# Low-part score products over 128 rows in place of 64, in a hybrid attention encoder on one Trainium2 core

## The chip, the cores and the metric

The kernel runs on one core of one Trainium2 chip. The metric is device time of one execution in microseconds (us). Engines are called as in the profile: PE is TensorE (PEld its weight loads), DVE is VectorE, ACT is ScalarE, POOL is GpSimd, SP is SyncE, which issues the DMAs here.

## What is computed

Two layers, each with three attention branches side by side over 512 tokens of width 1024. Two of the branches matter here, the banded one (8 heads on 2 key/value heads, 64 wide, each query block of 128 sees its own and its neighbour blocks) and the differential one (4 heads, two components of 64 each):

```python
def swa_branch(q, k, v, sink, bias_band):
    ...
    s = jnp.einsum('bnqgrd,bnkgd->bngrqk', q, kb).astype(jnp.float32) * SWA_HEAD_DIM ** -0.5
    s = s + bias_band.reshape(SWA_KV_HEADS, SWA_GROUP, BLOCK, 3 * BLOCK)[None, None]
    ...
    m = jnp.maximum(jnp.max(s, axis=-1, keepdims=True), sink_l)
    p = jnp.exp(s - m)
    p = p / (jnp.sum(p, axis=-1, keepdims=True) + jnp.exp(sink_l - m))
    ...

def diff_branch(q, k, v, lam_q1, lam_k1, lam_q2, lam_k2, g_sub, rel_bias, lam_init):
    ...
        s = jnp.einsum('bqhcd,bkhcd->bchqk', qb, k).astype(f32) * d ** -0.5 + bias[None, None]
        p = jax.nn.softmax(s, axis=-1)
        a = p[:, 0] - lam * p[:, 1]
        return jnp.einsum('bhqk,bkhe->bqhe', a.astype(v.dtype), v)
    ...

for l in range(DEPTH):
    ...
    o_a = (mla_branch(...) * jax.nn.silu(za)) @ w_o_mla[l]
    o_b = (swa_branch(qb_, kb_, vb_, sink[l], swa_bias) * jax.nn.silu(zb)) @ w_o_swa[l]
    o_c = (diff_branch(...) * jax.nn.silu(zc)) @ w_o_diff[l]
    y = (g[:, :, 0] * o_a + g[:, :, 1] * o_b + g[:, :, 2] * o_c) @ w_out[l]
    x = x + gate * rms_norm(y, g_post[l])
```

## The kernel before

Every float32 operand of a product is split in two parts that PE takes as float32r: a high part, the rounded copy made by ACT (`act_copy`, L81), and a low part, the rest, made by DVE (`sub`, L84). A product is then three matmuls into one PSUM tile (`mm3`, L86 to L89): high by high, high by low, low by high. A weight unit (`wunit`, L100) is a DMA of 512 KB into a `wr` tile (2 buffers), ACT's split into `wh` and DVE's into `wl` (3 buffers each). A projection (`proj_T`, L451) takes one unit and 24 matmuls of 512 columns.

The scores of the two branches have heads of only 64 rows, half of PE's height, and use it so: `stack_q` (L786) puts the high query of a head in one half of the 128 partitions and its low part in the other half; `stack_k` (L798) puts the high key in both halves, the second by a DVE copy (L802). One matmul over 128 rows is then high key by high query plus high key by low query. The third term, low key by high query, is a second matmul into the same score tile over the 64 rows of the high query alone.

- Banded branch (`swa_attention`, L839): for 2 key heads, 4 query blocks and 4 query heads, L866 is the first product and L867 the second, 256 columns wide for the outer blocks and 384 for the inner ones: 32 pairs per layer. The low key is made in `swa_kv` (L822), which also copies it into the other half (L823), since a key head serves query heads of both halves.
- Differential branch (`diff_attention`, L923): for 4 heads, 4 query tiles and 2 components, L939 is the first product and L940 the second, 512 columns: 32 pairs per layer. The low keys of both components share one tile `kl`, a half each, made in `diff_qkv` (L905, L916).

Score tiles rotate through 2 PSUM buffers (`sc`). DVE adds the bias and takes the maximum (L868, L941), ACT the exponential (L874, L946), POOL scales (L882, L950). Then `second` transposes the probabilities (L691) and multiplies them by the values (L700 to L704, `mm3`). Queries and keys lie in tiles of the tag `op`, a ring of 12 buffers; a differential head took 5 of them (2 queries, 2 high keys, 1 for the low keys).

The order of the instructions on each engine is fixed when the program is built, by a scheduler that works with estimated times and with the priorities set in the code (`tc.high_priority`); between the score products stand projections, merges (`merge_steps`) and, in layer 0, pieces of the next layer's modulation (`mod_late`, `mod_rows`), whose weights go through the same `wr` ring.

Of the kernel before, what the change touches and what calls it, by code (L numbers as in the profile page):

```python
# [12 lines left out]
F32R = mybir.dt.float32r  # L13
# [4 lines left out]
P = 128  # L18
S = 512
# [31 lines left out]
def hybrid_kernel(ctx, tc, x, c, w_ada, b_ada, g_pre, g_post, w_in, g_q, w_uq, g_kv, w_ukv,  # L51
# [6 lines left out]
    pe, act, dve, pool, sp = nc.tensor, nc.scalar, nc.vector, nc.gpsimd, nc.sync  # L58
# [4 lines left out]
    def T(tag, shape, dt=F32, bufs=None):  # L63
        count[0] += 1
        return sb.tile(shape, dt, tag=tag, name=f"{tag}_{count[0]}",
                       bufs=bufs or BUFS.get(tag, 1))

    def stat(n):
        return T("st", [P, n], F32, 24)
# [3 lines left out]
    def Q(tag):  # L73
        count[0] += 1
        return ps.tile([P, S], F32, tag=tag, name=f"ps_{tag}_{count[0]}", bufs=PB[tag])

    def f(ap):
        return ap.bitcast(F32)

    def act_copy(out_, in_, scale=1.0):  # L80
        return act.activation(out=out_, in_=in_, func=AF.Copy, scale=scale)  # L81

    def sub(out_, a, b, eng=None):
        return (eng or dve).tensor_tensor(out=out_, in0=a, in1=b, op=ALU.subtract)  # L84
# [69 lines left out]
    for k, src, n in ((PR_GQ, g_q, 2), (PR_GKV, g_kv, 1), (PR_GSUB, g_sub, 1)):  # L154
        pool.dma_start(out=prm[1][k - 32:k - 32 + n * DEPTH, :],
                       in_=src.rearrange("l (a b) -> (l a) b", b=P))
# [118 lines left out]
    def bg_step(n=1):  # L275
        for _ in range(n):
            if bg and next(bg[0], bg) is bg:
                bg.clear()
# [163 lines left out]
    def skewed(d2, pitch, n):  # L442
        a = d2[0:1, :]
        return bass.AP(tensor=a.tensor, offset=a.offset + 127, ap=[[pitch, P], [1, n]])
# [243 lines left out]
    def transposed_block(blocks):  # L688
        tr = Q("tr")
        for i, b in enumerate(blocks):  # L690
            pe.transpose(tr[:, i * P:(i + 1) * P], b, ident)  # L691
        ph = T("pt", [P, S], F32R)
        pl = T("pt", [P, S], F32R)
        act_copy(ph, tr)
        sub(pl, tr, f(ph))
        return ph, pl
# [142 lines left out]
    def swa_attention(l, qs, kk, vt):  # L839
        o_all = []  # L840
        bt = []

        def first(idx):
            g, n = idx // NT, idx % NT
            kh, kl = kk[g]
            if n == 0:
                bt.clear()
                for i in range(2):
                    b = T("x5", [P, 896])
                    for h in range(2):  # L850
                        sp.dma_start(out=b[:, h * 384:(h + 1) * 384],
                                     in_=skewed(bias_s[4 * g + 2 * i + h], 511, 384))
                    bt.extend([b[:, 0:384], b[:, 384:768]])
                o_all.extend(T("o", [P, S]) for _ in range(2))
            k0, k1 = max(n - 1, 0), min(n + 2, NT)
            j0 = (k0 - n + 1) * P
            w = (k1 - k0) * P
            mx, sm, nm, sk, rr = (stat(4) for _ in range(5))
            pr = T("p", [P, NT, S])
            for i in range(4):  # L860
                q = qs[4 * g + i]
                hi = slice((i % 2) * 64, (i % 2) * 64 + 64)
                s = Q("sc")
                ts_ = slice(n * P, (n + 1) * P)
                ks_ = slice(k0 * P, k1 * P)
                pe.matmul(s[:, :w], q[:, ts_], kh[:, ks_], start=True, stop=False)  # L866
                pe.matmul(s[:, :w], q[hi, ts_], kl[hi, ks_], start=False, stop=True)  # L867
                dve.tensor_tensor_reduce(  # L868
                    out=pr[:, i, :w], in0=s[:, :w], in1=bt[i][:, j0:j0 + w], scale=1.0,
                    scalar=sinkt[:, l * 8 + 4 * g + i:l * 8 + 4 * g + i + 1],  # L870
                    op0=ALU.add, op1=ALU.max, accum_out=mx[:, i:i + 1])
                dve.tensor_scalar(out=nm[:, i:i + 1], in0=mx[:, i:i + 1], scalar1=-1.0,
                                  scalar2=None, op0=ALU.mult)
                act.activation(out=pr[:, i, :w], in_=pr[:, i, :w], func=AF.Exp,  # L874
                               bias=nm[:, i:i + 1], accum_out=sm[:, i:i + 1])
            dve.tensor_tensor(out=sk, in0=sinkt[:, l * 8 + 4 * g:l * 8 + 4 * g + 4], in1=nm,
                              op=ALU.add)
            act.activation(out=sk, in_=sk, func=AF.Exp)
            dve.tensor_tensor(out=sk, in0=sk, in1=sm, op=ALU.add)
            dve.reciprocal(out=rr, in_=sk)  # L880
            for i in range(4):
                pool.tensor_scalar(out=pr[:, i, :w], in0=pr[:, i, :w], scalar1=rr[:, i:i + 1],  # L882
                                   scalar2=1.0, op0=ALU.mult, op1=ALU.mult)
            return pr

        def second(idx, pr):
            g, n = idx // NT, idx % NT
            ob = o_all[2 * g:2 * g + 2]
            k0, k1 = max(n - 1, 0), min(n + 2, NT)
            av = Q("av")  # L890
            for kb in range(k0, k1):
                ph, pl = transposed_block([pr[:, i, (kb - k0) * P:(kb - k0 + 1) * P]
                                           for i in range(4)])
                av_step(av, vt[:, kb * 2 + g], ph, pl, kb == k0, kb == k1 - 1)
            ol = T("ta", [P, S])
            act_copy(ol[0:64], av[64:128])
            for i in range(4):
                dve.tensor_tensor(out=ob[i // 2][(i % 2) * 64:(i % 2) * 64 + 64, n * P:(n + 1) * P],
                                  in0=av[0:64, i * P:(i + 1) * P],
                                  in1=ol[0:64, i * P:(i + 1) * P], op=ALU.add)  # L900

        pipelined(first, second, 2 * NT)
        return o_all

    def diff_qkv(l, hd, hh, hl):  # L905
        bg_step()
        qq = stack_q(l, C_QC + hd * P, hh, hl)
        bg_step()
        kh = [T("op", [P, S], F32R) for _ in range(2)]
        kl = T("op", [P, S], F32R)  # L910
        ka = proj_T(l, C_KC + hd * P, hh, hl)
        for i in range(2):
            stack_k(ka, i, kh[i])
        for i in range(2):
            hi = slice(i * 64, i * 64 + 64)
            sub(kl[hi], ka[hi], f(kh[i][hi]))  # L916
        vt = T("big", [P, 2, S], F32R)
        tr = v_transposed(proj_T(l, C_VC + hd * P, hh, hl))
        act_copy(vt[:, 0], tr)
        sub(vt[:, 1], tr, f(vt[:, 0]))  # L920
        return qq, kh, kl, vt

    def diff_attention(l, hh, hl, fill):  # L923
# [3 lines left out]
        def first(hd):  # L927
            qq, kh, kl, vt = ops[hd]
            b = T("x5", [P, 896])
            sp.dma_start(out=b, in_=skewed(bias_d[hd], 1023, 896))  # L930
            pr = T("p", [P, NT, S])
            for t in range(NT):
                ts_ = slice(t * P, (t + 1) * P)
                mx, nm, sm, rr = (stat(2) for _ in range(4))
                pc = [pr[:, t], T("ta", [P, S])]
                for i in range(2):
                    hi = slice(i * 64, i * 64 + 64)
                    s = Q("sc")
                    pe.matmul(s, qq[i][:, ts_], kh[i], start=True, stop=False)  # L939
                    pe.matmul(s, qq[i][hi, ts_], kl[hi], start=False, stop=True)  # L940
                    dve.tensor_tensor_reduce(out=pc[i], in0=s, in1=b[:, 384 - t * P:896 - t * P],  # L941
                                             scale=1.0, scalar=-3.0e38, op0=ALU.add, op1=ALU.max,
                                             accum_out=mx[:, i:i + 1])
                    dve.tensor_scalar(out=nm[:, i:i + 1], in0=mx[:, i:i + 1], scalar1=-1.0,  # L944
                                      scalar2=None, op0=ALU.mult)
                    act.activation(out=pc[i], in_=pc[i], func=AF.Exp, bias=nm[:, i:i + 1],  # L946
                                   accum_out=sm[:, i:i + 1])
                dve.reciprocal(out=rr, in_=sm)
                dve.tensor_tensor(out=rr[:, 1:2], in0=rr[:, 1:2], in1=lam_neg[l], op=ALU.mult)
                pool.tensor_scalar(out=pc[1], in0=pc[1], scalar1=rr[:, 1:2], scalar2=1.0,  # L950
                                   op0=ALU.mult, op1=ALU.mult)
                dve.scalar_tensor_tensor(out=pc[0], in0=pc[0], scalar=rr[:, 0:1], in1=pc[1],
                                         op0=ALU.mult, op1=ALU.add)
            return pr
# [244 lines left out]
```

## Time and profile before

| what | us |
|---|---|
| median of 3 timed runs | 1256.59 (1256.41 to 1256.79) |
| span of the profiled execution | 1256.0; its time with what lies around the span isn't listed apart |
| PE matmul L87, L88, L89 into `ps_dn` from `hT` (840 each) | 339.8, 336.3, 335.7 |
| PE transposes L691 (544) | 94.1 |
| DVE weight splits L84 `wl` (141) | 179.5 |
| ACT weight splits L81 `wh` (141) | 149.1 |

The page divides the span in 40 slices; these rows give the busy share of each engine in tenths, and the clock that PE was granted in tenths of full speed:

```profile
PE   5898999999999999999999999999999999999997
DVE  7864676986765577665567558778765557766553
PEclk8899999999999999999999999999999999999999
```

The banded branch of layer 0 lies in slices 8 to 12, the differential one in 14 to 18; layer 1 follows from slice 21 on. A row of a timeline gives start, duration, engine, line, operation, output <- inputs, rows*columns of the stationary operand, the moving operand's shape. Matmuls are pipelined, so the duration of one overlaps its neighbours, and the distance of two starts is the time that a matmul takes in the stream. "Idle before" is the time the engine stood still ahead of an instruction, with what ended it; "issue" there is idle time that ended with nothing the profile shows.

### The profile page before, as it was taken

The numbers are of one execution on the slowest core, as the hardware profiler recorded it, in microseconds if no ns is written. First come the engines' busy times: TensorE is split into PE (matmuls) and PEld (weight loads), VectorE is DVE, ScalarE is ACT, GpSimd is POOL, SyncE is SP. The second block draws the span as 40 slices with busy tenths as digits, with TensorE's granted clock in tenths as the row PEclk, the third lists the DMA queues.
The fourth block names the chain that finished last, engine by engine and source line by source line (L and its number), as shares of the span: only waits on it lengthen the run. The fifth ranks groups of instructions, "written<-read, shape, count | busy, mean of one in ns | idle before, by whom it ended". The sixth has DMA issues, their size and how long they took to land.

```text
span 1256.0 us, 15558 instructions
## 1 busy us (share of the span) xinstructions
PE 1216.1 (97%) x5428; PEld 944.4 (75%) x5428; DVE 837.2 (67%) x1732; ACT 632.2 (50%) x1250; POOL 188.3 (15%) x238
## 2 busy tenths in 40 slices
PE   5898999999999999999999999999999999999997
PEld 4776787767777767787878888887777876777786
DVE  7864676986765577665567558778765557766553
ACT  5454565545543446554357446564544345565431
POOL 4400211211110010001131001221121001000123
PEclk8899999999999999999999999999999999999999
DMA  9648431354355232334454433224422332223442
GB/s 317 186 123 233 118 99 55 102 149 143 94 144 160 77 85 70 96 96 137 133 173 132 110 92 87 63 80 134 126 68 81 100 93 74 82 84 86 142 156 95
DMA packets 169523, 146.86 MB, mean 117 GB/s; under 512 B 7679, under 2 KB 146999, under 8 KB 169444
## 3 DMA queue, kind: packets, MB, share of 16 engines
q1 hardware_dynamic: 169316, 145.85, 40.1%
q8 instruction: 43, 0.70, 0.2%
q14 instruction: 36, 0.29, 0.1%
q0 software_dynamic: 128, 0.01, 0.0%
HBM read 135.83 MB, written 14.20 MB: 119 GB/s over the span
## 4 chain that ended last, share of the span: by engine, by line
PE 81%; DVE 7%; DMA 6%; ACT 2%; POOL 2%; issue 1%; SPq 1%; DVEq 0%; POOLq 0%; ACTq 0%
PE ps_dn L87 18%; PE ps_dn L88 18%; PE ps_dn L89 18%; PE ps_tr L691 5%; DMA wr<-in_w_in 4%; PE ps_sc L940 2%; DVE o L202 2%; PE ps_sc L87 2%; PE ps_sc L89 2%; PE ps_sc L88 2%; PE ps_sc L867 2%; PE ps_av L701 1%; PE ps_av L700 1%; PE ps_sc L939 1%; DVE wl L84 1%
## 5 line engine op out<-in xcount | busy, mean ns | idle before, releaser
L87 PE MATMUL ps_dn<-hTh,wh 128*128 128x512 f32 x840 | 339.8, 404 | 2.6 <-ACT tf L479 1.8
L88 PE MATMUL ps_dn<-hTl,wh 128*128 128x512 f32 x840 | 336.3, 400 | 0.0
L89 PE MATMUL ps_dn<-hTh,wl 128*128 128x512 f32 x840 | 335.7, 400 | 0.4 <-DVE wl L84 0.4
L84 DVE TENSOR_TENSOR wl<-wr,wh 128x1024 fp32r<-128x1024 f32 x141 | 179.5, 1273 | 137.9 <-ACT wh L81 135.0
L81 ACT ACTIVATE wh<-wr 128x1024 fp32r<-128x1024 f32 x141 | 149.1, 1058 | 187.7 <-PE ps_dn L88 117.9
L87 PEld LDWEIGHTS ps_dn<-hTh,wh 128*128 128x128 f32 x840 | 158.3, 188 | 43.9 <-issue 6.4
L89 PEld LDWEIGHTS ps_dn<-hTh,wl 128*128 128x128 f32 x840 | 158.2, 188 | 38.3 <-issue 1.5
L88 PEld LDWEIGHTS ps_dn<-hTl,wh 128*128 128x128 f32 x840 | 158.3, 189 | 37.3 <-issue 2.8
L81 ACT ACTIVATE pt<-ps_tr 128x512 fp32r<-128x512 f32 x136 | 79.0, 596 | 91.9 <-PE ps_tr L691 91.2
L84 DVE TENSOR_TENSOR pt<-ps_tr,pt 128x512 fp32r<-128x512 f32 x136 | 92.1, 685 | 38.9 <-ACT pt L81 37.8
L691 PE MATMUL ps_tr<-ident,p 128*128 128x128 f32 x544 | 94.1, 275 | 1.0 <-POOL p L762 1.0
L762 POOL TENSOR_SCALAR p<-p,st 128x512 f32<-128x512 f32 x64 | 49.0, 783 | 291.2 <-DVE st L760 254.0
L691 PEld LDWEIGHTS ps_tr<-ident,p 128*128 128x128 f32 x544 | 68.9, 141 | 23.9 <-issue 3.3
L87 PE MATMUL ps_dn<-u,wh 128*128 128x512 f32 x192 | 77.4, 403 | 1.8 <-DVE x L298 1.8
L89 PE MATMUL ps_dn<-u,wl 128*128 128x512 f32 x192 | 77.3, 402 | 0.0
L88 PE MATMUL ps_dn<-u,wh 128*128 128x512 f32 x192 | 77.2, 402 | 0.0
L950 POOL TENSOR_SCALAR ta<-ta,st 128x512 f32<-128x512 f32 x32 | 22.9, 716 | 338.0 <-DVE st L944 207.4
L882 POOL TENSOR_SCALAR p<-p,st 128x256 f32<-128x256 f32 (+1 forms) x64 | 38.2, 616 | 185.9 <-DVE st L880 161.2
L758 ACT ACTIVATE p<-ps_sc,st 128x512 f32<-128x512 f32 x64 | 43.8, 686 | 36.3 <-DVE st L757 36.0
L757 DVE TENSOR_REDUCE st<-ps_sc 128x1 f32<-128x512 f32 x64 | 43.4, 686 | 15.8 <-PE ps_sc L89 15.4
L87 PEld LDWEIGHTS ps_dn<-u,wh 128*128 128x128 f32 x192 | 36.1, 188 | 11.7 <-DVE x L298 2.6
L868 DVE CUSTOM_DVE_ANT_0 p<-ps_sc,x,sinkt 128x256 f32<-128x256 f32 (+1 forms) x64 | 34.0, 545 | 16.2 <-PE ps_sc L867 12.0
(345 smaller groups left out, 2119.8 us busy)
## 6 DMA issues: line engine op xcount, KB each, us to landing
wr<-in_w_in SPq DMA_DIRECT2D x105, 512.0 KB, 3.9
wr<-in_w_ada SPq DMA_DIRECT2D x32, 512.0 KB, 3.7
wr<-in_w_out SPq DMA_DIRECT2D x16, 512.0 KB, 3.7
big<-in_w_ada SPq DMA_DIRECT2D x10, 512.0 KB, 9.3
big<-in_x SPq DMA_DIRECT2D x8, 512.0 KB, 4.9
wr<-in_w_o_mla SPq DMA_DIRECT2D x8, 512.0 KB, 3.6
wr<-in_w_o_swa SPq DMA_DIRECT2D x8, 512.0 KB, 3.5
wr<-in_w_o_diff SPq DMA_DIRECT2D x8, 512.0 KB, 3.4
```

Source lines behind the costliest of these rows:

```text
L81: return act.activation(out=out_, in_=in_, func=AF.Copy, scale=scale)
L84: return (eng or dve).tensor_tensor(out=out_, in0=a, in1=b, op=ALU.subtract)
L87: pe.matmul(o, ah, bh, start=start, stop=False)
L88: pe.matmul(o, ah, bl, start=False, stop=False)
L89: pe.matmul(o, al, bh, start=False, stop=stop)
L202: end = dve.scalar_tensor_tensor(out=acc, in0=src[k], scalar=cact[:, k:k + 1], in1=acc, op0=ALU.mult, op1=ALU.add)
L691: pe.transpose(tr[:, i * P:(i + 1) * P], b, ident)
L757: dve.tensor_reduce(out=nm[:, t:t + 1], in_=s, axis=AX.X, op=ALU.max, negate=True)
L758: act.activation(out=pr[:, t], in_=s, func=AF.Exp, bias=nm[:, t:t + 1], accum_out=sm[:, t:t + 1])
L762: pool.tensor_scalar(out=pr[:, t], in0=pr[:, t], scalar1=rr[:, t:t + 1], scalar2=1.0, op0=ALU.mult, op1=ALU.mult)
L868: dve.tensor_tensor_reduce(out=pr[:, i, :w], in0=s[:, :w], in1=bt[i][:, j0:j0 + w], scale=1.0, scalar=sinkt[:, l * 8 + 4 * g + i:l * 8 + 4 ...
L882: pool.tensor_scalar(out=pr[:, i, :w], in0=pr[:, i, :w], scalar1=rr[:, i:i + 1], scalar2=1.0, op0=ALU.mult, op1=ALU.mult)
```

## The change

The second product of both branches runs over all 128 rows. In the banded branch that only drops the selection of rows, since the low key lay in both halves already. In the differential branch `kl` becomes two tiles, one per component, and a DVE copy puts each low key into the other half too: 2 more copies of 64x512 and 1 more `op` tile per head (6 in place of 5). With the low key in both halves, the second product also adds low key by low query, which the kernel before left out.

```diff
@@ swa_attention, first
             for i in range(4):
                 q = qs[4 * g + i]
-                hi = slice((i % 2) * 64, (i % 2) * 64 + 64)
                 s = Q("sc")
...
                 pe.matmul(s[:, :w], q[:, ts_], kh[:, ks_], start=True, stop=False)
-                pe.matmul(s[:, :w], q[hi, ts_], kl[hi, ks_], start=False, stop=True)
+                pe.matmul(s[:, :w], q[:, ts_], kl[:, ks_], start=False, stop=True)
@@ diff_qkv
         kh = [T("op", [P, S], F32R) for _ in range(2)]
-        kl = T("op", [P, S], F32R)
+        kl = [T("op", [P, S], F32R) for _ in range(2)]
...
         for i in range(2):
             hi = slice(i * 64, i * 64 + 64)
-            sub(kl[hi], ka[hi], f(kh[i][hi]))
+            lo = slice(64 - i * 64, 128 - i * 64)
+            sub(kl[i][hi], ka[hi], f(kh[i][hi]))
+            dve.tensor_copy(out=kl[i][lo], in_=f(kl[i][hi]))
@@ diff_attention, first
                 for i in range(2):
-                    hi = slice(i * 64, i * 64 + 64)
                     s = Q("sc")
                     pe.matmul(s, qq[i][:, ts_], kh[i], start=True, stop=False)
-                    pe.matmul(s, qq[i][hi, ts_], kl[hi], start=False, stop=True)
+                    pe.matmul(s, qq[i][:, ts_], kl[i], start=False, stop=True)
```

The change also moves instructions, from the start of the differential branch on; ahead of it no engine's order changes. Three places follow; lines of the banded branch are one lower in the code after, those of `diff_attention` are the same, and the new copy is L917.

First, PE at the first scores of head 0 in layer 0 (out <- moving, stationary; op_3712 and op_3713 are the queries, op_3752 and op_3753 the high keys, op_3754 and, after, op_3755 the low keys). Before:

```order
L89 MATMUL ps_dn_3799<-hTh_119,wl_3795 128x512
L939 MATMUL ps_sc_3965<-op_3752,op_3712 128x512
L939 MATMUL ps_sc_3971<-op_3753,op_3713 128x512
L940 MATMUL ps_sc_3965<-op_3754,op_3712 128x512
L87 MATMUL ps_dn_3844<-hTh_119,wh_3839 128x512
```

After, the same place:

```order
L89 MATMUL ps_dn_3802<-hTh_119,wl_3798 128x512
L939 MATMUL ps_sc_3971<-op_3752,op_3712 128x512
L939 MATMUL ps_sc_3977<-op_3753,op_3713 128x512
L87 MATMUL ps_dn_3847<-hTh_119,wh_3842 128x512
L88 MATMUL ps_dn_3847<-hTl_120,wh_3842 128x512
```

And after, 48 matmuls of two projections later:

```order
L89 MATMUL ps_dn_3889<-hTh_119,wl_3885 128x512
L940 MATMUL ps_sc_3971<-op_3754,op_3712 128x512
L940 MATMUL ps_sc_3977<-op_3755,op_3713 128x512
L87 MATMUL ps_dn_3929<-hTh_119,wh_3924 128x512
L88 MATMUL ps_dn_3929<-hTl_120,wh_3924 128x512
```

The first second product moved behind these two projections, to where the second one of the same tile pair stood before.

Second, DVE at the keys of head 0 in layer 0, from the copies of the high key on. Before:

```order
L802 CAST op_3752<-op_3752 64x512
L802 CAST op_3753<-op_3753 64x512
L84 TENSOR_TENSOR op_3754<-ps_dn_3761,op_3752 64x512
L84 TENSOR_TENSOR op_3754<-ps_dn_3761,op_3753 64x512
L941 ISA p_3959,st_3960<-ps_sc_3965,x_869_3957 128x512
L941 ISA st_3960 128x1
L84 TENSOR_TENSOR wl_3919<-wr_3917,wh_3918 128x1024
```

After:

```order
L802 CAST op_3752<-op_3752 64x512
L802 CAST op_3753<-op_3753 64x512
L84 TENSOR_TENSOR op_3754<-ps_dn_3762,op_3752 64x512
L84 TENSOR_TENSOR op_3755<-ps_dn_3762,op_3753 64x512
L917 CAST op_3754<-op_3754 64x512
L917 CAST op_3755<-op_3755 64x512
L84 TENSOR_TENSOR wl_3925<-wr_3923,wh_3924 128x1024
```

The two new copies stand in the place that the first bias step (L941) held, ahead of a weight split; that step went behind it.

Third, ACT where head 2 of layer 0 takes its first `op` tiles (op_4256 before, op_4262 after), beside the last exponentials (L946) of head 0 (p_3959 before, p_3965 after) and the first of head 1. Before:

```order
L946 ACTIVATE p_3959,st_4025<-p_3959,st_4024 128x512
L946 ACTIVATE ta_4027,st_4025<-ta_4027,st_4024 128x512
L946 ACTIVATE p_4103,st_4106<-p_4103,st_4105 128x512
L81 ACTIVATE wh_4335<-wr_4334 128x1024
L81 ACTIVATE op_4256<-ps_dn_4264 64x512
```

After:

```order
L946 ACTIVATE p_3965,st_4031<-p_3965,st_4030 128x512
L946 ACTIVATE ta_4033,st_4031<-ta_4033,st_4030 128x512
L81 ACTIVATE wh_4344<-wr_4343 128x1024
L81 ACTIVATE op_4262<-ps_dn_4270 64x512
L946 ACTIVATE p_4109,st_4112<-p_4109,st_4111 128x512
```

In both, the last exponential of head 0 stands ahead of head 2's first copy; the first exponential of head 1 moved behind that copy. On SP one pair of loads swaps in each layer: a load of `g_post` (L297) now stands ahead of the last unit of `w_o_diff`; POOL's order is as before.

## The prediction

> **What bounds the kernel now.** I read four views in this order: the page's shares by engine, its chain of work that ended last, the busy time by stage, and the list of what TensorE (PE) waited for.
>
> ```profile
> span 1256.0 us, 15558 instructions
> PE 1216.1 (97%) x5428; PEld 944.4 (75%) x5428; DVE 837.2 (67%) x1732; ACT 632.2 (50%) x1250; POOL 188.3 (15%) x238
> PE 81%; DVE 7%; DMA 6%; ACT 2%; POOL 2%; issue 1%; SPq 1%; DVEq 0%; POOLq 0%; ACTq 0%
> ```
>
> PE is busy for 97% of the span and holds 81% of the chain that ended last. That could still hide a stage where another engine decides, so I cut out the stages that hold the two score loops. The rows give the stretch, then PE, PEld, DVE, ACT and POOL busy time, the granted clock, the DMA share and GB/s. The first two are banded attention of layer 0 (its start, then the rest), then differential attention of layer 0, banded and differential attention of layer 1.
>
> ```profile
> 243.00:268.00 25.00, 23.15 (x113) 17.11 (x111) 20.64 (x45) 12.15 (x24) 4.38 (x7) 1.00 0.49 129
> 268.00:352.00 84.00, 84.00 (x375) 62.37 (x375) 62.74 (x171) 41.67 (x96) 15.02 (x26) 0.98 0.45 128
> 407.00:536.00 129.00, 129.00 (x538) 92.37 (x537) 87.67 (x207) 70.78 (x126) 10.77 (x15) 1.00 0.30 84
> 851.00:956.00 105.00, 105.00 (x469) 77.36 (x468) 75.82 (x196) 53.50 (x120) 17.51 (x28) 1.00 0.38 107
> 1007.00:1135.00 128.00, 128.00 (x534) 91.51 (x533) 86.37 (x203) 69.76 (x125) 10.76 (x15) 1.00 0.29 82
> PE ps_sc L866 <- DVE st L868: 1.8, 2, 1.0
> ```
>
> In four of the five PE is busy without a gap and DVE has between a quarter and a third of its time free. Only at 243 to 268 us does PE stand idle, 1.85 us, and the last row, from the waits of PE over 235 to 310 us, says for whom: DVE's reduction L868. So in four stretches a nanosecond less on PE should be a nanosecond off the span; the first has another bound.
>
> **What a second product costs.** "Busy" does not tell whether PE works at its pace. The starts of its matmuls do. Layer 0, differential attention, PE alone, start and duration:
>
> ```profile
> 430.43 0.39 PE L89 MATMUL ps_dn<-hTh,wl 128*128 128x512 f32 x1
> 430.66 0.40 PE L87 MATMUL ps_dn<-hTh,wh 128*128 128x512 f32 x1
> 430.90 0.39 PE L939 MATMUL ps_sc<-op,op 128*128 128x512 f32 x1
> 431.22 0.49 PE L940 MATMUL ps_sc<-op,op 64*128 64x512 f32 x1
> 431.64 0.50 PE L88 MATMUL ps_dn<-hTl,wh 128*128 128x512 f32 x1
> 431.98 0.40 PE L89 MATMUL ps_dn<-hTh,wl 128*128 128x512 f32 x1
> ```
>
> The regular step from start to start is (430.90 - 430.43) / 2 = 0.235 us for 512 columns; each matmul overlaps its neighbours. Around the 64-row product of L940 the steps are 0.32 ahead of it, 0.42 behind it and 0.34 behind its successor. From 430.90 to 431.98 that is 1.08 us in place of 3 x 0.235 = 0.705, so one such product costs 0.375 us more than a full-height one at the same place. Is it all of them, and is it a wait?
>
> ```profile
> L940 PEld LDWEIGHTS ps_sc<-op,op 64*128 64x128 f32 x64 | 11.7, 183 | 21.4 <-issue 21.4
> L867 PEld LDWEIGHTS ps_sc<-op,op 64*128 64x128 f32 x64 | 11.8, 184 | 14.3 <-issue 12.2
> L939 PEld LDWEIGHTS ps_sc<-op,op 128*128 128x128 f32 x64 | 12.0, 190 | 2.7 <-issue 1.0
> L940 PE MATMUL ps_sc<-op,op 64*128 64x512 f32 x64 | 31.7, 496 | 0.0
> L939 PE MATMUL ps_sc<-op,op 128*128 128x512 f32 x64 | 25.8, 414 | 0.0
> ```
>
> All 64 of L940 have it (21.4 us of idle weight load, none of it for a semaphore: "issue"), while the full-height L939 in the same loop has 1.0. The weight load of the 64-row product starts only with its own matmul, that of the others one step ahead.
>
> Here two rules of the Trainium skill stand against each other. "TensorEngine Tiling (Array Packing)", Key Properties, says that changing the tiling mode drains the engine; by it a 64-row product pays one drain on the way in and one on the way out, and the trace's 0.32, 0.42 and 0.34 agree. "TensorE: Matmul & The Clock Gate", LDWEIGHTS (loading the stationary operand), says that a weight load takes its time from the columns and not from the rows; 183 against 190 ns agrees, and by that rule alone doubling the rows would change nothing on PE, which is the second rival below.
>
> **The sum.** Differential attention has 64 second products (4 heads, 4 query tiles, 2 components, 2 layers): 64 x 0.375 = **24.0 us**. Banded attention has 32 of 384 columns and 32 of 256. One of each kind, in layer 1:
>
> ```profile
> 880.52 0.33 PE L866 MATMUL ps_sc<-op,op 128*128 128x384 f32 x1
> 880.79 0.44 PE L867 MATMUL ps_sc<-op,op 64*128 64x384 f32 x1
> 881.16 0.50 PE L88 MATMUL ps_dn<-hTl,wh 128*128 128x512 f32 x1
> 881.50 0.40 PE L700 MATMUL ps_av<-pt,big 128*128 128x512 f32 x1
> ...
> 915.17 0.28 PE L866 MATMUL ps_sc<-op,op 128*128 128x256 f32 x1
> 915.38 0.38 PE L867 MATMUL ps_sc<-op,op 64*128 64x256 f32 x1
> 915.70 0.38 PE L866 MATMUL ps_sc<-op,op 128*128 128x256 f32 x1
> 916.01 0.38 PE L867 MATMUL ps_sc<-op,op 64*128 64x256 f32 x1
> 916.32 0.45 PE L703 MATMUL ps_av<-pt,big 128*64 128x512 f32 x1
> 916.60 0.39 PE L704 MATMUL ps_av<-pt,big 128*128 128x512 f32 x1
> 916.84 1.04 PE L691 MATMUL ps_tr<-ident,p 128*128 128x128 f32 x8
> ```
>
> At 384 columns: 881.50 - 880.52 = 0.98 us, against (2 x 384 + 512) / 512 x 0.235 = 0.59, so 0.39 each, 32 x 0.39 = **12.5 us**. At 256 columns: 916.60 - 915.17 = 1.43 us for two products and the step after them, against (4 x 256 + 512) / 512 x 0.235 = 0.705, so 0.36 each, 32 x 0.36 = **11.5 us**. That takes for granted that a 256-column step can be 0.118 us, with a full weight load in each. The last row bears on it: eight transposes with eight 128-row weight loads take at most 1.04 us, 0.13 each. If 0.13 were the floor, 64 matmuls of 256 columns would lose 0.012 us each, 0.8 us; the bound from below is nothing. I take nothing. Together 24.0 + 12.5 + 11.5 = **48.0 us** less on PE.
>
> **What does not reach the end.** The chain ahead of 268 us in layer 0, in order of time:
>
> ```profile
> 259.01 5.21 DMA wr<-in_w_in
> ...
> 266.84 0.50 DVE p L868
> ...
> 267.41 0.44 PE ps_sc L866
> L867 PE MATMUL ps_sc<-op,op x6: 379/382/439, 243.4 to 262.1; 64*128 64x256 f32 x4, 64*128 64x384 f32 x2
> ```
>
> Up to 267.4 us it runs over a weight load and DVE, not over PE. Six second products lie ahead of that point (last row); what they save, 4 x 0.36 + 2 x 0.39 = **2.2 us**, turns into a longer wait of PE for L868. Elsewhere PE leads, and I set off **1 us** for handovers that become late, with an end below at 0 and one above in the first rival.
>
> **What is added.** Sixteen copies on DVE (one per component, head and layer). Nearest is the copy of the high key, of the same shape:
>
> ```profile
> L802 DVE CAST op<-op x20: 419/422/820, 222.7 to 1102.7; 64x512 fp32r<-64x512 f32 x20
> wr<-in_w_o_diff SPq DMA_DIRECT2D x8, 512.0 KB, 3.4
> ```
>
> 16 x 0.42 = 6.7 us of DVE, 3.4 per layer, beside differential stages where DVE has 129.00 - 87.67 = 41 us free. On the path they would cost at most 6.7 us. In the order they stand right behind the subtractions, ahead of one weight split, and the first second product now stands 48 matmuls later, 48 x 0.235 = 11.3 us, which covers the 0.84 us of two copies thirteen times over. Were that cover gone, that one product would wait up to 0.84 us in each layer, with all of PE's work queued behind it. I take nothing. The move itself costs nothing: the same matmuls stand there in another order, and the first scores of head 0 come 11 us later, but its last ones at the same place. On SP a load of g_post goes ahead of the last unit of w_o_diff in each layer; such a unit takes 3.4 us to land (second row), so a delay of about that is the upper end, and two split units ahead of it, 24 matmuls of 0.235 us each, cover it: nothing. In banded attention the low key was already held twice, so nothing is added there and no row moves.
>
> The operand ring "op" has 12 buffers; a head took 5 and now takes 6, so two heads fill it and head 2 must wait for head 0 to be read out. In ACT's order the last exponential of head 0 stands ahead of head 2's first copy, so the tiles are free when that is reached: nothing.
>
> So 48.0 - 2.2 - 1.0 = 44.8 us off. The page's span of 1256.0 us is 0.6 us under the median of the runs, 1256.59, and I take that margin as unchanged: 1256.6 - 44.8 = **1211.8**, say 1212 us.
>
> **The rivals.** First, **DVE becomes the bound in banded attention**. At 243 to 268 us it was busy 20.64 of 25 us, 83%, and PE waited. Taking 10 us from 268 to 352 and 12 from 851 to 956 raises its share to 62.74 / 74 = 85% and 75.82 / 93 = 82%, just there. If every stretch then behaves like the first, all 24 us of banded attention are lost: 1256.6 - 24.0 + 1.0 = 1234 us; half of it gives about 1222. Against it: the 83% came with a chain over a 5.21 us load, which the later stretches do not have; the differential stages reach only (87.67 + 3.4) / 117 = 78%. I give 0.05 to the whole and 0.12 to a part.
>
> Second, **the gaps are not from the row count**, but from the pair of products into one score tile or from their operands; then they stay at 128 rows: 1256.6 us, no change. This also covers that the change does not do on the chip what it says. Against it: L87 to L89 are three products into one tile too and keep 0.235 us. Chance 0.04.
>
> Third, **slower**: head hd+2's first copy on ACT waits, in the ring, for the last score of head hd. Behind it in ACT's order stand weight splits, which wait too, and PE runs dry. There are four such places (heads 2 and 3 of each layer); to end 0.2% (2.5 us, about what a measurement of this kernel can tell from no change) above the time before, each has to stall PE for more than (44.8 + 2.5) / 4 = 11.8 us, for instance 13 us, giving 1256.6 - 44.8 + 52 = 1264 us. It decides from the point where that copy comes more than 11.8 us before the last score; the order has it behind. Chance 0.02.
>
> **How the numbers follow.** The forecast, 1208 to 1217 us, has 0.73; more than the sum 0.04. The low end is the whole 48.0 with 5% for the reading of steps, 1256.6 - 50.4 = 1206; the high end takes in the half of the first rival, 1222, with 2 us of the copies not hidden, 1224. Faster by over 0.2%: 0.73 + 0.04 + 0.17 = 0.94; within it 0.04; slower 0.02.
>
> **What would show it.** In the profile after, the second products should read 128*128, the step behind them 0.235 us at 512 columns, their "issue" idle near L939's 1.0 us, and PE's busy time some 48 us lower. The wait for L868 ahead of 268 us should grow from 1.8 to about 4 us. I am wrong if the steps stay at 0.3 to 0.4 us (second rival), if PE's busy time falls but its waits for DVE in banded attention grow by 10 us or more (first), or if ACT's copies for heads 2 and 3 show long waits for scores (third).

## The result and the profile after

| | before | after |
|---|---|---|
| median, us | 1256.5 (1255.61 to 1256.79, 4 runs) | 1210.37 (1208.57 to 1210.71, 4 runs) |
| span of the profiled execution, us | 1256.0 | 1206.8 (that execution took 1208.57) |

The ratio is 0.9629, with a 95% interval of 0.9615 to 0.9642: 46 us off, between 45.0 and 48.4 by the interval. The forecast was 1212, 44.8 us off.

The page after: span, shares by engine, and the chain that ended last.

```profile
span 1206.8 us, 15578 instructions
PE 1165.8 (97%) x5428; PEld 946.0 (78%) x5428; DVE 840.5 (70%) x1748; ACT 632.2 (52%) x1250; POOL 194.7 (16%) x238
PE 79%; DMA 7%; DVE 7%; issue 2%; POOL 2%; ACT 2%; SPq 1%; DVEq 0%; POOLq 0%; ACTq 0%
```

PE has as many matmuls as before and is busy 50.3 us less; DVE has 16 instructions and 3.3 us more. PE still holds 97% of the span.

The second products in the groups by shape (L940 in differential attention, L866 in banded attention, where all lines are one lower now): busy time, mean in ns, idle before and its releaser.

```profile
L866 PEld LDWEIGHTS ps_sc<-op,op 128*128 128x128 f32 x64 | 12.2, 191 | 1.5
L940 PEld LDWEIGHTS ps_sc<-op,op 128*128 128x128 f32 x64 | 12.1, 189 | 2.6
L940 PE MATMUL ps_sc<-op,op 128*128 128x512 f32 x64 | 25.5, 404 | 0.0
```

The "issue" idle of 21.4 and 12.2 us is gone, and the mean of L940 fell from 496 to 404 ns. The steps, in PE's timeline of the same profile, at 384 and at 256 columns in layer 1:

```profile
852.72 0.33 PE L865 MATMUL ps_sc<-op,op 128*128 128x384 f32 x1
852.89 0.34 PE L866 MATMUL ps_sc<-op,op 128*128 128x384 f32 x1
853.06 0.39 PE L88 MATMUL ps_dn<-hTl,wh 128*128 128x512 f32 x1
853.29 0.40 PE L700 MATMUL ps_av<-pt,big 128*128 128x512 f32 x1
...
872.90 0.28 PE L865 MATMUL ps_sc<-op,op 128*128 128x256 f32 x1
873.01 0.28 PE L866 MATMUL ps_sc<-op,op 128*128 128x256 f32 x1
873.13 0.28 PE L865 MATMUL ps_sc<-op,op 128*128 128x256 f32 x1
873.25 0.28 PE L866 MATMUL ps_sc<-op,op 128*128 128x256 f32 x1
873.37 0.40 PE L88 MATMUL ps_dn<-hTl,wh 128*128 128x512 f32 x1
```

At 384 columns the step is 0.17 us, at 256 columns 0.47 / 4 = 0.118, weight load included. Three steps that took 0.98 us now take 0.57.

Where did the 49.2 us of span come off? The first and last start of a line tell it. Banded attention by its first product (L866 before, L865 after), differential attention by its second (L940), each layer before, then after:

```profile
L866 PE MATMUL ps_sc<-op,op x32: 277/338/442, 243.2 to 350.9; 128*128 128x256 f32 x16, 128*128 128x384 f32 x16
L866 PE MATMUL ps_sc<-op,op x32: 277/338/445, 851.6 to 953.7; 128*128 128x256 f32 x16, 128*128 128x384 f32 x16
L940 PE MATMUL ps_sc<-op,op x32: 490/497/502, 407.8 to 533.7; 64*128 64x512 f32 x32
L940 PE MATMUL ps_sc<-op,op x32: 491/497/502, 1007.8 to 1133.7; 64*128 64x512 f32 x32
```

```profile
L865 PE MATMUL ps_sc<-op,op x32: 277/333/686, 242.2 to 339.1; 128*128 128x256 f32 x16, 128*128 128x384 f32 x16
L865 PE MATMUL ps_sc<-op,op x32: 277/333/422, 826.7 to 917.4; 128*128 128x256 f32 x16, 128*128 128x384 f32 x16
L940 PE MATMUL ps_sc<-op,op x32: 387/394/481, 407.4 to 509.9; 128*128 128x512 f32 x32
L940 PE MATMUL ps_sc<-op,op x32: 387/394/482, 982.5 to 1085.0; 128*128 128x512 f32 x32
```

| stretch | lead at its start, us | lead at its end | gained | forecast |
|---|---|---|---|---|
| banded, layer 0 | 243.2 - 242.2 = 1.0 | 350.9 - 339.1 = 11.8 | 10.8 | 12.0 - 2.2 = 9.8 |
| on to the end of differential, layer 0 | 11.8 | 533.7 - 509.9 = 23.8 | 12.0 | 12.0 |
| banded, layer 1 | 851.6 - 826.7 = 24.9 | 953.7 - 917.4 = 36.3 | 11.4 | 12.0 |
| on to the end of differential, layer 1 | 36.3 | 1133.7 - 1085.0 = 48.7 | 12.4 | 12.0 |

The lead grows in these four stretches and hardly elsewhere; 1.0 us of it was there ahead of the first changed instruction and belongs to the two executions, not to the change. The banded rows end at the first product of the last pair, so they hold 31 of the 32 second products of a layer, 11.6 us of PE's work and not 12.0.

At the one place where PE waited before, two views of the profile after: the waits of PE over 235 to 310 us, and the first products of the seventh and the ninth banded pair in PE's timeline.

```profile
PE ps_sc L865 <- DVE st L867: 2.7, 1, 2.7
...
266.38 0.34 PE L865 MATMUL ps_sc<-op,op 128*128 128x384 f32 x1
272.63 0.33 PE L865 MATMUL ps_sc<-op,op 128*128 128x384 f32 x1
```

The same two products before:

```profile
267.41 0.44 PE L866 MATMUL ps_sc<-op,op 128*128 128x384 f32 x1 [0.82 <-DVE st L868]
275.95 0.33 PE L866 MATMUL ps_sc<-op,op 128*128 128x384 f32 x1
```

PE now waits 2.7 us for the bias step. The seventh pair starts 267.41 - 266.38 = 1.0 us earlier than before, the lead that was there at the first pair. That looks as if nothing of the first six products had come through, but the granted clock has to be read with it. Busy time and clock over 252 to 264 and 264 to 276 us (PE, PEld, DVE, ACT, POOL, granted clock, DMA share, GB/s), before, then after:

```profile
252.00:264.00 12.00, 10.97 (x54) 7.96 (x53) 9.53 (x21) 5.98 (x12) 0.00 (x0) 1.00 0.61 162
264.00:276.00 12.00, 11.18 (x49) 8.38 (x47) 8.81 (x23) 5.92 (x13) 1.84 (x4) 0.86 0.49 146
```

```profile
252.00:264.00 12.00, 9.30 (x40) 7.32 (x40) 9.57 (x20) 5.93 (x12) 0.00 (x0) 0.86 0.59 152
264.00:276.00 12.00, 12.00 (x64) 10.19 (x63) 11.16 (x30) 6.92 (x16) 1.84 (x4) 1.00 0.51 155
```

Both executions have one spell at a lower clock, of the same size (0.86 over 12 us). Before, it comes behind the start of the seventh pair (the prediction's row up to 268 us has a clock of 1.00); after, it comes ahead of it. At the ninth pair, with the spell behind both, the lead is 275.95 - 272.63 = 3.3 us, so 2.3 us were gained over eight pairs, against 2.2 + 2 x 0.39 = 3.0 us of PE's work. About 0.7 us were lost there, and 11.6 - 10.8 = 0.8 by the end of the stretch, near the 0.9 us by which the wait grew.

### The profile page after: what moved, and what is told of

Same layout as the page of the kernel before. It is cut to its first block, busy times and chain, and to the rows that moved or that the text cites. A ratio compares the mean times of both kernels' runs of the same rounds, so it can differ in the third digit from the quotient of the medians.

```text
span 1206.8 us, 15578 instructions
## 1 busy us (share of the span) xinstructions
PE 1165.8 (97%) x5428; PEld 946.0 (78%) x5428; DVE 840.5 (70%) x1748; ACT 632.2 (52%) x1250; POOL 194.7 (16%) x238
## 4 chain that ended last, share of the span: by engine, by line
PE 79%; DMA 7%; DVE 7%; issue 2%; POOL 2%; ACT 2%; SPq 1%; DVEq 0%; POOLq 0%; ACTq 0%
PE ps_dn L87 18%; PE ps_dn L89 18%; PE ps_dn L88 18%; PE ps_tr L691 5%; DMA wr<-in_w_in 3%; PE ps_sc L87 2%; PE ps_sc L89 2%; PE ps_sc L88 2%; PE ps_av L700 1%; PE ps_av L701 1%; PE ps_sc L939 1%; PE ps_sc L940 1%; DVE wl L84 1%; DMA wr<-in_w_ada 1%; PE ps_pj L87 1%
## 5 line engine op out<-in xcount | busy, mean ns | idle before, releaser
L87 PE MATMUL ps_dn<-hTh,wh 128*128 128x512 f32 x840 | 336.2, 400 | 1.7 <-ACT tf L479 1.1
L762 POOL TENSOR_SCALAR p<-p,st 128x512 f32<-128x512 f32 x64 | 48.6, 778 | 291.1 <-DVE st L760 237.6
L950 POOL TENSOR_SCALAR ta<-ta,st 128x512 f32<-128x512 f32 x32 | 26.6, 833 | 313.9 <-DVE st L949 197.5
L881 POOL TENSOR_SCALAR p<-p,st 128x256 f32<-128x256 f32 (+1 forms) x64 | 41.4, 665 | 161.9 <-DVE st L879 116.0
L873 ACT ACTIVATE p<-p,st 128x256 f32<-128x256 f32 (+1 forms) x64 | 35.6, 556 | 20.9 <-DVE st L871 20.2
```

Source lines behind the costliest of these rows:

```text
L87: pe.matmul(o, ah, bh, start=start, stop=False)
L762: pool.tensor_scalar(out=pr[:, t], in0=pr[:, t], scalar1=rr[:, t:t + 1], scalar2=1.0, op0=ALU.mult, op1=ALU.mult)
```

## The experiments

Theory: a matmul over 64 rows costs PE about 0.38 us in lengthened steps, and PE sets the pace everywhere but ahead of 268 us. The rivals: the gain came from the new order or the copies; DVE is the bound in banded attention; any matmul below full height is slow. In each diff "-" is the kernel named in the sentence ahead.

**One part alone.** First the banded part, as an edit of the kernel before:

```diff
-                pe.matmul(s[:, :w], q[hi, ts_], kl[hi, ks_], start=False, stop=True)
+                pe.matmul(s[:, :w], q[:, ts_], kl[:, ks_], start=False, stop=True)
```

> The kernel before with the full-height second product in banded attention alone; no instruction is added and no order should move. Theory (each 64-row matmul costs PE three lengthened steps, 0.36 to 0.39 us in all, and PE sets the pace): 24.0 - 2.2 us off, 1256.5 to about 1234.5 us, the steps around the second product of the differential branch still 0.32, 0.42 and 0.34. Rival (DVE decides in banded attention, and what the changed kernel gained came from the new order of the differential branch): at most 12 us off, 1244 us or more.

Measured: 1233.08 us, ratio 0.9807 (0.9791 to 0.9822) to 1257.45 in the same session: 24.3 us off, 22.4 to 26.3. The differential products kept their cost, as the weight load shows (this kernel's groups by shape; the second product is on L939 here):

```profile
L939 PEld LDWEIGHTS ps_sc<-op,op 64*128 64x128 f32 x64 | 11.7, 183 | 21.4 <-issue 21.4
```

So the banded part needs neither copies nor a new order for its gain, and "12 us at most" falls.

Then the differential part, as an edit of the changed kernel:

```diff
-                pe.matmul(s[:, :w], q[:, ts_], kl[:, ks_], start=False, stop=True)
+                hi = slice((i % 2) * 64, (i % 2) * 64 + 64)
+                pe.matmul(s[:, :w], q[hi, ts_], kl[hi, ks_], start=False, stop=True)
```

> The changed kernel with the 64-row second product put back in banded attention alone. Theory: 64 x 0.375 = 24.0 us off, 1256.5 to about 1232.5 us, and the gains of this run and of the banded part alone add up to that of the changed kernel, 46 us. Rival (the two parts share a limit, DVE or the weight ring): the two gains add up to clearly more than 46 us, so each alone over 23.5.

Measured: 1231.45 us, ratio 0.9791 (0.9777 to 0.9806), 26.3 us off, 24.4 to 28.0. Each part alone gave 2 us more than forecast, and their sum, 50.6 us, is above the 46 of the changed kernel. In the same session the near twin of the changed kernel (96 rows, below) was 48.7 us off (46.5 to 50.7). The profiles allow a closer look, from the first banded product of layer 0 to the last differential one of layer 1, so without what lies ahead of the change. Before, that takes 1133.7 - 243.2 = 890.5 us. The banded part alone takes 22.6 us less (241.3 to 1109.2), the differential part alone 23.8 less (241.9 to 1108.6), the changed kernel 47.7 less (242.2 to 1085.0). So the parts add up, 46.4 against 47.7, and no shared loss shows; of the difference, over a microsecond fits the clock, which was lower for longer in the profile of the banded part (0.91 over 240 to 276 us, against 0.95 before, after and in the other part). Of the 2 us above the forecast, 1.9 and 1.3 us stand, in these profiles, ahead of the first banded product, where nothing was changed.

**The copies without the rows.** The changed kernel, with two low-key tiles per head, the copies and the fuller ring, but the differential product over its own 64 rows:

```diff
-                    pe.matmul(s, qq[i][:, ts_], kl[i], start=False, stop=True)
+                    pe.matmul(s, qq[i][i * 64:i * 64 + 64, ts_], kl[i][i * 64:i * 64 + 64], start=False, stop=True)
```

> The changed kernel (two low-key tiles per head, the copies, the fuller ring of tiles) with the second product of the differential branch over 64 rows again; banded attention at full height. Theory: the copies and the ring cost nothing, so the time is that of the banded part alone, about 1234.5 us. Rival (the added copies or the ring cost time that the faster matmuls pay for): up to 6.7 us more, 1241 us.

Measured: 1232.78 us, ratio 0.9805 (0.9789 to 0.982), beside 1233.08 without copies. The copies and the sixth tile cost nothing that shows, and bring nothing by themselves. In this kernel no product reads the copied half, and the first second product kept its place (other instructions did move); that its move is free rests on the changed kernel's own gain of 12.0 and 12.4 us there.

**Is it the height or the half?** The changed kernel with 96 rows for component 0 (32 rows of low by low are left out there):

```diff
-                    pe.matmul(s, qq[i][:, ts_], kl[i], start=False, stop=True)
+                    n = 96 if i == 0 else 128
+                    pe.matmul(s, qq[i][0:n, ts_], kl[i][0:n], start=False, stop=True)
```

> The changed kernel with the second product of component 0 of the differential branch over 96 rows (64 rows of low key by high query and 32 of low by low; the other 32 rows of low by low are left out), 32 matmuls. Theory A (the gap comes with a half-height tile of the array, which 96 rows do not fit): as the changed kernel, 1210.4 us, step 0.235 us. Theory B (any matmul below full height loses its overlap): 32 x 0.375 = 12 us more, 1222 us, with steps of 0.32, 0.42 and 0.34 around the 96-row products.

Measured: 1209.15 us, ratio 0.9613 (0.9597 to 0.963). PE's timeline of this kernel:

```profile
414.10 0.39 PE L939 MATMUL ps_sc<-op,op 128*128 128x512 f32 x1
414.33 0.40 PE L941 MATMUL ps_sc<-op,op 96*128 96x512 f32 x1
414.57 0.40 PE L939 MATMUL ps_sc<-op,op 128*128 128x512 f32 x1
414.81 0.40 PE L941 MATMUL ps_sc<-op,op 128*128 128x512 f32 x1
```

The steps ahead of and behind the 96-row product are 0.23 and 0.24 us, those of any full matmul. Theory B falls: it is not the unused rows that cost time. Nor does every smaller stationary operand cost it. One of 64 columns over all 128 rows, among full ones in the changed kernel (L701, 128*64), starts at 854.35 us, 0.24 behind the matmul ahead of it and 0.23 ahead of the next.

**One visit or one matmul?** The changed kernel with the 64-row product issued twice (the term counts double):

```diff
-                    pe.matmul(s, qq[i][:, ts_], kl[i], start=False, stop=True)
+                    for h in range(2):
+                        r = slice(i * 64, i * 64 + 64)
+                        pe.matmul(s, qq[i][r, ts_], kl[i][r], start=False, stop=h == 1)
```

> The changed kernel with the second product of the differential branch over its 64 rows again, and issued twice in a row over the same rows (the low key by high query counts double). Theory A (only the change between full and half height drains the array): the second of the two costs a plain step, 64 x 0.235 = 15 us above the same kernel with one such product (about 1234.5), 1249.5 us, step between the two 0.235 us. Theory B (a 64-row matmul never overlaps its neighbours, alike or not): 64 x 0.42 = 27 us above, 1261 us, step between the two 0.42 us.

Measured: 1252.43 us, ratio 0.9963 (0.9951 to 0.9976); by the ratios 0.0158 x 1257 = 20 us above the kernel with one, give or take about 2.5, between the two theories. The timeline and the weight load of this kernel show why:

```profile
414.68 0.40 PE L939 MATMUL ps_sc<-op,op 128*128 128x512 f32 x1
415.01 0.73 PE L942 MATMUL ps_sc<-op,op 64*128 64x512 f32 x2
415.67 0.50 PE L87 MATMUL ps_dn<-hTh,wh 128*128 128x512 f32 x1
416.01 0.39 PE L88 MATMUL ps_dn<-hTl,wh 128*128 128x512 f32 x1
...
419.36 0.50 PE L942 MATMUL ps_sc<-op,op 64*128 64x512 f32 x1
419.79 0.50 PE L89 MATMUL ps_dn<-hTh,wl 128*128 128x512 f32 x1
420.22 0.50 PE L942 MATMUL ps_sc<-op,op 64*128 64x512 f32 x1
420.65 0.50 PE L87 MATMUL ps_dn<-hTh,wh 128*128 128x512 f32 x1
...
  issue: 23.6, 73
  DVE op L84: 0.4, 1
```

Side by side, two 64-row products take 416.01 - 414.68 = 1.33 us with the step ahead and the one behind, against 4 x 0.235 = 0.94: 0.39 us too much, the same as one product alone. But the scheduler put other matmuls between the two in 10 of the 64 cases, and there every step is 0.43, and the cost is paid twice. With 54 x 0.235 + 10 x (0.235 + 0.375) that gives 18.8 us, near the 20. The weight load stands idle 74 times ahead of such a product (73 ended by "issue", one by DVE), once for each of the 54 + 2 x 10 = 74 visits, not 128 times. So the price is of the visit, as theory A has it, but its step between the two, expected at 0.235, is not plain. The row "x2" hides the second start; a narrower window of the timeline gives it, and the weight loads around it tell more:

```profile
415.35 0.39 PE L942 MATMUL ps_sc<-op,op 64*128 64x512 f32 x1
...
415.01 0.29 PEld L942 LDWEIGHTS ps_sc<-op,op 64*128 64x128 f32 x2 [0.36 <-issue]
415.67 0.19 PEld L87 LDWEIGHTS ps_dn<-hTh,wh 128*128 128x128 f32 x1 [0.37 <-issue]
```

The steps are 0.33 into the first 64-row product, 0.34 from it to the second, 0.32 out of the second and 0.34 behind. Read so, each change of height, in or out, lengthens the step ahead of it by about 0.09 us and the step behind it by about 0.10, 0.19 in all, and a visit has two changes: 0.38. A lone product has both on its own step, 0.235 + 0.10 + 0.09 = 0.425, and 0.42 or 0.43 was measured. At both changes the weight load starts only with its own matmul (415.01 and 415.67 us); between the two 64-row products both loads are done by 415.30, ahead of the second start. Two products in different halves of the array were not tried.

"TensorEngine Tiling (Array Packing)" in the Trainium skill, Key Properties, has the drain at a change of tiling mode and not of the tile; 96 rows without a gap, and a cost that comes with the change of height and not with each 64-row product, agree with it. Whether a change of tile alone is free no run here shows.

**Is PE still the bound in banded attention?** The changed kernel without the second product there:

```diff
-                pe.matmul(s[:, :w], q[:, ts_], kh[:, ks_], start=True, stop=False)
-                pe.matmul(s[:, :w], q[:, ts_], kl[:, ks_], start=False, stop=True)
+                pe.matmul(s[:, :w], q[:, ts_], kh[:, ks_], start=True, stop=True)
```

> The changed kernel without any second product in banded attention (low key by query is left out there). Theory (PE still sets the pace there with 64 matmuls less): 32 x 0.175 + 32 x 0.118 = 9.4 us off, less about 0.7 us ahead of 268 us where a load and DVE decide, 1210.4 to about 1201.5 us. Rival (DVE, 83 to 85% busy there, is by now the bound): under 3 us off, 1207.5 us or more, and PE's waits for the bias step of DVE grow by some 6 us.

Measured: 1199.48 us, ratio 0.9542 (0.9527 to 0.9556): by the ratios 0.0087 x 1256.6 = 10.9 us below the changed kernel, or 10.0 by that kernel's ratio in its later session (0.9622, below), each give or take about 2.5. That is the forecast of 9.4 - 0.7 = 8.7 within the error, and clearly more than the rival's 3, so DVE is not the bound there even with 64 matmuls less; the first rival falls in all but the first 25 us. The waits of PE in this kernel over 200 to 420 us name DVE four times, for 3.3 us in all; in the changed kernel it was 3.1. In the profiles, the stretch from the first banded product to the last differential one is 7.3 us shorter than in the changed kernel (835.5 against 842.8), at a clock of 0.91 against 0.95 over 240 to 276 us, an estimated 1.4 us of PE's work. The two longest of the four waits:

```profile
PE ps_av L700 <- DVE st L870: 1.5, 1, 1.5
PE ps_sc L865 <- DVE st L866: 1.4, 1, 1.4
```

**The first 25 us of banded attention.** There PE waits, and part of the gain was lost. In layer 0 the modulation of layer 1 is computed on DVE in eight steps (`mod_late`), which `MPOS` places; five of them come in a burst. Two other placements beside the changed kernel, on one chip:

```diff
-    MPOS = (5, 6, 7, 8, 9, 10, 11, 12)
+    MPOS = (2, 3, 4, 5, 11, 12, 13, 14)
```

```diff
-    MPOS = (5, 6, 7, 8, 9, 10, 11, 12)
+    MPOS = (5, 11, 12, 13, 14, 15, 16, 17)
```

> The changed kernel as it is, on the chip of the next two, for comparison: 46 us off, about 1210.5 us; PE waits some 2.7 us for the bias step ahead of 268 us.

> The changed kernel with the eight steps of next-layer modulation in layer 0 (a 512 KB load and two DVE multiply-adds each) one at a time from the third early gate on, where before five of them came in one burst ahead of the banded attention. Theory (what the six second products ahead of 268 us save is lost to that burst on DVE and the load ring): PE's wait for the bias step there goes from 2.7 us to under 1, and the time falls by 2 to 4 us against the changed kernel, to about 1207.5 us. Rival (DVE is full from 220 us on whatever the place of these steps, or the gates then wait for their weights): within 1 us of the changed kernel, the wait only elsewhere.

> The same with the eight steps at the sixth early gate, the later gates and the queries of the banded attention, so later on average than in the run above. Theory: between the two, 1 to 3 us off. Rival: as above, within 1 us of the changed kernel.

| | median, us | ratio to before |
|---|---|---|
| changed again | 1207.69 | 0.9622 (0.9608 to 0.9635) |
| modulation early | 1217.94 | 0.9694 (0.9679 to 0.9709) |
| modulation spread | 1206.05 | 0.9608 (0.9595 to 0.9621) |

The changed kernel again waited 2.4 us there. Early placing missed by 10 us: it took that wait away and put larger ones elsewhere (the two longest waits of PE, 100 to 420 us, in that kernel):

```profile
PE ps_dn L87 <- ACT wh L81: 5.2, 1, 5.2
PE ps_sc L87 <- ACT p L758: 2.8, 2, 2.6
```

In the two profiles (1218.9 us against 1205.9 for the changed kernel beside it) PE is idle 7.5 us more, and busy 5.5 us more for the same matmuls, at a clock of 0.988 against 0.992.

With the later spread, PE has no gap in the stretch from 242 to 267 us and its full clock; below it stands the same stretch of the changed kernel, from the profile after.

```profile
242.00:267.00 25.00, 25.00 (x130) 20.67 (x129) 21.32 (x50) 14.32 (x29) 1.84 (x4) 1.00 0.49 134
```

```profile
242.00:267.00 25.00, 22.30 (x116) 18.35 (x115) 21.59 (x46) 12.20 (x24) 5.25 (x8) 0.93 0.54 141
```

The spell of lower clock did not go away, though: it now lies between 100 and 120 us (0.91 there, against 1.00 in the changed kernel beside it). Its time is 1.6 us below the changed kernel by the medians, and each of its four times is below each of that kernel's four (1207.36 us at most against 1207.52 at least), but the intervals of the ratios overlap; it is the fastest complete version here, by an amount that these runs can't be sure of.

## Why the prediction was right

- **PE sets the pace in four of the five stretches**: shown. The lead grows there by 46.6 us in all (table), and another 10 to 11 us come off by the ratios (7.3 in the profiles) when PE loses 64 matmuls more in banded attention.
- **0.375, 0.39 and 0.36 us per product, 48.0 us in all**: shown by the steps after, by the 50.3 us that PE is busy less, and by each part alone (24.3 us against 24.0 - 2.2 = 21.8, and 26.3 against 24.0; in the profiles 1.9 and 1.3 us of that lie ahead of the change). The price belongs to the two changes of height that make one visit, which the prediction did not separate from the matmul itself. Its reading that only the 64-row product's weight load is late was half of it: the load of the full-height matmul behind it is late too, as the run with two products shows.
- **A 256-column step can be 0.118 us**: shown, 0.47 us for four. The floor of 0.13 does not exist.
- **2.2 us lost ahead of 268 us**: right in place, too large in size. The growth of the wait was put at 2.2 us, to about 4; it measured 0.9, to 2.7. The lead at the ninth pair and at the end of the stretch says that 0.7 to 0.8 us were lost, so most of what the six products save did reach the end. The median came out 1.3 us better than the forecast (46.1 us off against 44.8), about what this term was too large by.
- **1 us for late handovers**: hardly seen. The four stretches gave 46.6 of the 48.0 us, and 0.7 to 0.8 of the rest is the loss ahead of 268 us; about 0.6 is left, part of it behind the last start that was compared.
- **Copies, moved instructions and ring at nothing**: shown for copies and ring (1232.78 against 1233.08); for the moved instructions argued from the gains of 12.0 and 12.4 us in the stretches that hold them.
- **The rivals**: DVE as the bound fell with the run without second products; the row count as no cause fell with the steps; the stall in the ring did not show, since the lead grew by 12.0 and 12.4 us in the differential stretches, where it would have stood.

## What to carry to other kernels

Where PE sets the pace, read the distance between matmul starts, not the busy share: a matmul that uses half of the array's rows among full ones showed as "busy" and cost 0.36 to 0.39 us more than a full one. If the idle rows can hold something harmless (here the low key twice), fill them; 96 rows were enough. Where such matmuls have to stay, put them next to each other, since the price was for going to half height and back: two on the same rows cost it once. And when two profiles are compared at one point, look whether a spell of lower clock lies ahead of that point in one and behind it in the other.

## What was not expected of the hardware

Between two 64-row products side by side the step was 0.34 us, neither the plain 0.235 nor the 0.42 that leads out of a single one, while the total of a visit stayed at 0.39 us. A change of height lengthens the step on either side of it, and this step has one such side. And POOL's scaling in differential attention (L950, 32 of 128x512) took longer though it does the same work: mean 716 ns before, 833 after. With the copies but 64-row products it was 753, and 696 with each of these issued twice, so the copies alone don't bring it. What slows it was not tried; it does not show in the time, since the only wait of PE for POOL in the profile after is 0.8 us, for another line (L762).
